# Making an MLP's summed weight factors ahead, behind the mixer blocks' last products

## The chip, the cores and the metric

One core of a Trainium2 chip runs the kernel, in one launch. The metric is the device time of one execution in microseconds, median of several runs; lower is better. Engines go by the profile's names: PE (TensorE), PEld (its weight loads), DVE (VectorE), ACT (ScalarE), POOL (GpSimd) and SP (SyncE, which here issues transfers and nothing else).

## The reference, cut to what matters

```python
def reference(x, meta_tokens, w_in, ...):
    h = jnp.concatenate([meta, x], axis=1)          # 16 + 2048 rows, 1024 wide, float32
    for i in range(DEPTH):                          # DEPTH = 1
        xn = rmsnorm(h, norm_mix_w[i])
        z, xbc, dt_raw, u_s5, gates = jnp.split(xn @ w_in[i], IN_SPLITS, axis=-1)
        y_a = ssd_branch(z, xbc, dt_raw, ...)       # chunked state-space scan, 16 heads
        y_b = s5_branch(u_s5, ...)                  # S5 scan, then y @ w_glu, val * sigmoid(gate)
        g_a, g_b = jnp.split(jax.nn.sigmoid(gates), 2, axis=-1)
        h = h + (g_a * y_a + g_b * y_b) @ w_out[i]
        hn = rmsnorm(h, norm_mlp_w[i])
        h = h + jnp.square(jax.nn.relu(hn @ w_ff_in[i])) @ w_ff_out[i]   # 1024 -> 4096 -> 1024
    return rmsnorm(h, final_norm_w)[:, N_META:]
```

## The kernel before, in words

Every product in float32 is made of three products of a rounded part ("h", "high") and a remainder ("l", "low"): `mm3` (L243 to L245) does high by high, high by low and low by high. So each operand has to be split first: ACT copies it rounded, DVE or POOL subtracts the copy from it.

**Mixer blocks.** The 2048 rows go in four blocks of 512 (`for b in range(NB)`). A block runs through "units" of weights, 1 MB each when split: 16 for the convolved inputs and 16 for the gates of the SSD part, 8 for the mixing gates (`gb`), 8 for `w_glu` and 8 for `w_out`. `rhs_group` takes units one by one, does 24 matmuls for each, and calls `evac` for the results of the last one. Three buffers hold units (`NWU`): `get` issues a unit's load when the unit two before it begins. In block 0 a unit comes raw from the inputs by SP's queue, is split by ACT and POOL (L216, L217) and is stored to DRAM by SP (L225); in blocks 1 to 3 POOL's queue reads it split (`wu<-wsd`, L227). The last two parts of a block are the GLU products (four groups of two units; `evac_glu`, L1261 to L1266, takes the results with ACT, DVE and POOL) and the output products (two groups of four; `evac_out`, L1296 to L1301, adds x and stores h to DRAM). Beside them DVE and ACT make the next block's normalized rows (L261 to L277), and in the last block the MLP's first rows. Memory of the block's SSD part (`ssd%d`) is given back before the GLU part's pool (`glu%d`) is opened.

**The MLP** multiplies by a scheme of seven products in place of eight for each 2 by 2 block of matrices (Strassen's, in Winograd's form). Rows go in three blocks of 768, 768 and 512 (`FB`), each through eight steps (`di`). A step has 28 products: twice seven for `w_ff_in` (`ff_in`) and twice seven for `w_ff_out` (`ff_out`), each with a weight factor. Of the seven factors of a group, three are quarters of the weights as they are and four are sums of quarters.

Class `Weights` supplies the factors. In the first block `make` loads a group's two raw tiles by SP (512 KB each), lets POOL add up the four sums (L1366 to L1369 and L1380 to L1383), and `weight` splits each factor (copy by ACT, L1341; subtraction by DVE or POOL as the string `ENG` says, L1342) into a tile `wc` and stores it to DRAM (`wcd<-wc`, L1343). Three tiles `wc` (`wcs`) and one factor ahead of the product (`AHEAD`) are all there is in that block: a tile comes free when its product and its store are done. In the second and third block `read` fetches the factors from DRAM by POOL's queue (`wc<-wcd` and `wr<-wcd`, L1352) into those tiles and four more.

**Order.** Engines run their queues in order. A planner sets that order: it simulates the program and gives an engine the instruction that is ready, in program order among those that are. `tc.issue_after(mm)` puts what is written under it behind the product `mm`, for instructions of that product's engine, TensorE. A `pool` is a stack of memory on one side of the chip's SBUF: tiles of a new pool wait for the tiles that had the same memory.

Of the kernel before, what the change touches and what calls it, by code (L numbers as in the profile page):

```python
# [9 lines left out]
F32 = mybir.dt.float32  # L10
F32R = mybir.dt.float32r
# [24 lines left out]
NWC = 5  # L36
NWU = 3
NJK = 1
AHEAD = 1
NRAW = 4  # L40
FPACE = 2
# [85 lines left out]
def _body(ctx, tc, d, out):  # L127
# [759 lines left out]
        return t  # L887


    xp = pool("xn", stack=xp_st)  # L890

    def load_x(pl, r0, L, src):
# [193 lines left out]
    for b in range(NB):  # L1086
# [166 lines left out]
            xn = make_xn(gp, b + 1, xp)  # L1253
        mh = gp.tile([P, 8, TB], F32R, name="mixh")
        ml = gp.tile([P, 8, TB], F32R, name="mixl")
        for q in range(4):
            n = q // 2

            def evac_glu(c, p):
                th = gp.tile([P, 256], F32, name="gth", tag="gth", bufs=2)  # L1260
                S.activation(th, p[:, 256:512], AF.Tanh, scale=0.5)  # L1261
                V.scalar_tensor_tensor(th, th, 1.0, p[:, 0:256], op0=ALU.add, op1=ALU.mult)
                o = (q % 2) * 256
                V.scalar_tensor_tensor(th, sgbs[n][:, c, o:o + 256], 1.0, th, op0=ALU.add, op1=ALU.mult)
                ma = mixA[:, c, q * 256:(q + 1) * 256]
                G.tensor_tensor(ma, ma, th, op=ALU.add)  # L1266
            rhs_group([(b, U_GLU + q * 2 + i) for i in range(2)], y5h, y5l, evac_glu)
            if q % 2 == 0:
# [10 lines left out]
        if b == NB - 1:  # L1279
            y5_st.close()  # L1280
            mp_st.close()
            xp_st.close()
            cm_st.close()
            fw = pool("mlpw")
            hp = pool("mlpx", stack=hp_st)
            hn = x_factors(hp, FB[0][1] // 2)
            rows = ff_norm(split_into(hn), lambda nm: ff_raw(fw, nm),
                           lambda nm: ff_sum(fw, nm).rearrange("p (f l) -> p f l", f=4), bank, NE[0],
                           FB[0][0], FB[0][1] // 2, 1)
            for _ in rows:  # L1290
                pass
        for n in range(2):
            def evac_out(c, p, n=n, b=b):
                r0 = b * TB + c * P
                xr = gp.tile([P, 512], F32, name="xr", tag="xr", bufs=2)
                nc.sync.dma_start(xr, d["x"][r0:r0 + P, n * 512:(n + 1) * 512])  # L1296
                V.tensor_tensor(xr, xr, p, op=ALU.add)
                nc.sync.dma_start(h2d[r0:r0 + P, n * 512:(n + 1) * 512], xr)
                jk = gp.tile([P, 512], F32, name="jk", tag="jk", bufs=2)
                i = b * NC4 + c  # L1300
                S.activation(jk, xr, AF.Square, accum_out=ssh[:, n, i:i + 1])  # L1301
            rhs_group([(b, U_OUT + n * 4 + i) for i in range(4)], mh, ml, evac_out)
        if b < NB - 1:
            V.tensor_tensor(ssh[:, 0, b * NC4:(b + 1) * NC4], ssh[:, 0, b * NC4:(b + 1) * NC4],
                            ssh[:, 1, b * NC4:(b + 1) * NC4], op=ALU.add)
            row_scale(ssh[:, 0, b * NC4:(b + 1) * NC4], rsh[:, b * NC4:(b + 1) * NC4], NC4)
        g_st.close()
        if b < NB - 1:
            y5_st.close()
# [13 lines left out]
    class Weights:  # L1323
# [14 lines left out]
        def weight(self, w, eng, n, i):  # L1338

            t = wcs[0].tile([P, 2, n, 512 // n], F32R, name="wc", tag="wc", bufs=wcs[1])  # L1340
            S.copy(t[:, 0], w)  # L1341
            (V if eng == "v" else G).tensor_tensor(t[:, 1], w, t[:, 0].bitcast(F32), op=ALU.subtract)  # L1342
            nc.sync.dma_start(wcd[i], t.rearrange("p a k n -> p (a k n)").bitcast(F32))  # L1343
            return t

        def read(self):
# [6 lines left out]
                    yield t.rearrange("p (a k n) -> p a k n", a=2, k=4 if j < 14 else 2)  # L1353

        def make(self):
            for di in range(ND):
                for half in range(2):
                    c = 2 * di + half
                    wa, wb = ff_raw(fw, "w1a"), ff_raw(fw, "w1b")
                    nc.sync.dma_start(wa, d["w"][U_FFI + 2 * c])  # L1360
                    nc.sync.dma_start(wb, d["w"][U_FFI + 2 * c + 1])
                    a11, a12, a21, a22 = [x.rearrange("p (a k n) -> p a k n", a=2, k=4)[:, i]
                                          for x in (wa, wb) for i in range(2)]
                    s2, s3, s1, s4 = [ff_sum(fw, nm).rearrange("p (k n) -> p k n", k=4)
                                      for nm in ("s2", "s3", "s1", "s4")]
                    G.tensor_tensor(s1, a21, a22, op=ALU.add)  # L1366
                    G.tensor_tensor(s2, s1, a11, op=ALU.subtract)
                    G.tensor_tensor(s3, a11, a21, op=ALU.subtract)
                    G.tensor_tensor(s4, a12, s2, op=ALU.subtract)  # L1369
                    for j, (w, e) in enumerate(zip((a11, s2, s3, a12, s1, a22, s4), ENG[half])):  # L1370
                        yield self.weight(w, e, 4, di * 28 + half * 7 + j)
                for n in range(2):
                    b1, b2 = ff_raw(fw, "w2a"), ff_raw(fw, "w2b")
                    nc.sync.dma_start(b1, d["w"][U_FFO + 4 * di + n])
                    nc.sync.dma_start(b2, d["w"][U_FFO + 4 * di + 2 + n])
                    b11, b12, b21, b22 = [x.rearrange("p (k a n) -> p k a n", k=2, a=2)[:, :, i, :]
                                          for x in (b1, b2) for i in range(2)]
                    t3, t1, t2, t4 = [ff_sum(fw, nm).rearrange("p (k n) -> p k n", k=2)
                                      for nm in ("t3", "t1", "t2", "t4")]
                    G.tensor_tensor(t3, b22, b12, op=ALU.subtract)  # L1380
                    G.tensor_tensor(t1, b12, b11, op=ALU.subtract)
                    G.tensor_tensor(t2, b22, t1, op=ALU.subtract)
                    G.tensor_tensor(t4, b21, t2, op=ALU.subtract)  # L1383
                    for j, (w, e) in enumerate(zip((b11, t3, b21, t4, t1, t2, b22), ENG[2 + n])):
                        yield self.weight(w, e, 2, di * 28 + 14 + n * 7 + j)

        def take(self):
            ahead = AHEAD if wcs[0] is fw and self.n == 0 else NRAW + wcs[1] - 2
# [373 lines left out]
```

## Time and profile before

| | us |
|---|---|
| median of 3 runs | 3317.12 (3313.74 to 3323.17) |
| the profiled execution's own time | 3315.93 |
| its span, first to last instruction | 3314.2 |
| PE busy | 3087.5 (93%) |
| DVE, POOL, ACT busy | 2119.2, 1417.8, 1227.8 |

In the profile's 40 slices of 83 us each (each digit is the busy share in tenths; PEclk the granted clock of TensorE, DMA the share of the 16 DMA engines), the mixer blocks fill slices 2 to 22, the MLP's first block 23 to 29:

```profile
PE   7989889998999999998999889898979999989998
DVE  8689999526844476426764577667675555475555
POOL 3356566523522244213442465665652222243343
PEclk9999989999999999999999999999999999999999
DMA  6376665775555654565756767777788888889998
```

A busy PE is not PE at its peak, and idle time of an engine that nothing waits for costs nothing; what counts is where PE waits.

### The profile page before, as it was taken

The page shows a single profiled execution, that of the slowest core. Times are in us where ns is not written, and L with a number is a line of the kernel's source. Part 1 is how long each engine was busy: PE and PEld are TensorE (multiplying, and loading weights), DVE is VectorE, ACT ScalarE, POOL GpSimd, SP SyncE. Part 2 cuts the span into 40 slices and gives each one's busy share as a digit, 9 for nine tenths or more (in the row PEclk, how much of TensorE's full clock was granted, in tenths as well). Part 3 has the DMA queues.
Part 4 walks back from the last instruction along what each step waited for, and adds up shares of the span by engine and source line. Part 5 has one row for each costly group of instructions (what it writes and reads, how often), then busy time and mean ns, then how long its engine had stood idle before and what let it go on. Part 6 is the DMA issues. An engine that isn't in the chain of part 4 may idle for free. (4 is left out here: it accounts for less than half of the span.)

```text
span 3314.2 us, 50076 instructions
## 1 busy us (share of the span) xinstructions
PE 3087.5 (93%) x18353; PEld 2747.0 (83%) x18353; DVE 2119.2 (64%) x4364; ACT 1227.8 (37%) x2569; POOL 1417.8 (43%) x1736
## 2 busy tenths in 40 slices
PE   7989889998999999998999889898979999989998
PEld 6678777887888778876788788888879999989998
DVE  8689999526844476426764577667675555475555
ACT  5354444434422443324433443334442121142222
POOL 3356566523522244213442465665652222243343
PEclk9999989999999999999999999999999999999999
DMA  6376665775555654565756767777788888889998
GB/s 225 117 220 172 186 168 170 280 248 185 171 197 187 220 156 168 204 229 179 226 174 210 275 254 268 261 272 267 268 292 282 248 248 247 247 286 369 360 358 279
DMA packets 299493, 776.56 MB, mean 234 GB/s; under 512 B 94736, under 2 KB 136848, under 8 KB 270448
## 3 DMA queue, kind: packets, MB, share of 16 engines
q0 software_dynamic: 88832, 411.21, 37.3%
q1 hardware_dynamic: 207808, 360.93, 33.0%
q8 instruction: 146, 2.39, 0.3%
q10 hardware_dynamic: 2608, 1.22, 0.1%
q14 instruction: 99, 0.81, 0.1%
HBM read 560.48 MB, written 214.88 MB: 234 GB/s over the span
## 5 line engine op out<-in xcount | busy, mean ns | idle before, releaser
L1501 DVE TENSOR_TENSOR acc<-acc,p 128x512 f32<-128x512 f32 x330 | 225.8, 684 | 167.0 <-PE p L245 164.8
L243 PE MATMUL pd<-hnh,wc 128*128 128x384 f32 (+1 forms) x896 | 291.2, 326 | 30.9 <-DMA wc<-wcd 20.6
L243 PE MATMUL pd<-wu,xnh 128*128 128x512 f32 x768 | 310.9, 405 | 4.0 <-DMA wu<-wsd 3.1
L245 PE MATMUL pd<-wu,xnl 128*128 128x512 f32 x768 | 310.5, 405 | 0.0
L244 PE MATMUL pd<-wu,xnh 128*128 128x512 f32 x768 | 309.5, 403 | 0.0
L245 PE MATMUL pd<-hnh,wc 128*128 128x384 f32 (+1 forms) x896 | 290.0, 327 | 14.2 <-DVE wc L1342 11.7
L244 PE MATMUL pd<-hnl,wc 128*128 128x384 f32 (+1 forms) x896 | 290.1, 324 | 0.0
L227 POOL DMA_DIRECT2D wu<-wsd x168 | 96.0, 572 | 374.2 <-PE pd L245 309.0
L243 PE MATMUL pd<-xnh,wu 128*128 128x512 f32 (+1 forms) x640 | 232.1, 363 | 9.0 <-DMA wu<-wsd 8.9
L1352 POOL DMA_DIRECT2D wr<-wcd x227 | 121.1, 534 | 273.7 <-PE pd L245 135.0
L244 PE MATMUL pd<-xnl,wu 128*128 128x512 f32 (+1 forms) x640 | 230.2, 360 | 0.0
L245 PE MATMUL pd<-xnh,wu 128*128 128x512 f32 (+1 forms) x640 | 229.9, 360 | 0.0
L1352 POOL DMA_DIRECT2D wc<-wcd x221 | 117.4, 531 | 254.5 <-PE pd L245 136.6
L243 PEld LDWEIGHTS pd<-hnh,wc 128*128 128x128 f32 x896 | 172.1, 192 | 36.4 <-ACT hnh L990 12.2
L749 DVE SCALAR_TENSOR_TENSOR cacc<-craw,conv,cacc 128x512 f32<-128x512 f32 (+1 forms) x192 | 172.1, 897 | 31.8 <-ACT cacc L746 27.1
L245 PEld LDWEIGHTS pd<-hnh,wc 128*128 128x128 f32 x896 | 172.1, 192 | 20.8 <-DVE wc L1342 15.0
L217 POOL TENSOR_TENSOR wu<-wst,wu 128x1024 fp32r<-128x1024 f32 x56 | 137.6, 2458 | 90.7 <-ACT wu L216 85.6
L243 PEld LDWEIGHTS pd<-wu,xnh 128*128 128x128 f32 x768 | 146.8, 191 | 34.9 <-DMA wu<-wsd 4.0
L245 PEld LDWEIGHTS pd<-wu,xnl 128*128 128x128 f32 x768 | 147.2, 192 | 31.6
L244 PEld LDWEIGHTS pd<-wu,xnh 128*128 128x128 f32 x768 | 147.1, 191 | 31.0 <-issue 0.2
L244 PEld LDWEIGHTS pd<-hnl,wc 128*128 128x128 f32 x896 | 172.2, 192 | 0.0
L243 PEld LDWEIGHTS pd<-xnh,wu 128*128 128x128 f32 x640 | 125.2, 196 | 26.1 <-issue 10.8
(1012 smaller groups left out, 9984.0 us busy)
## 6 DMA issues: line engine op xcount, KB each, us to landing
wu<-wsd POOLq DMA_DIRECT2D x168, 1024.0 KB, 5.2
wr<-wcd POOLq DMA_DIRECT2D x227, 512.0 KB, 5.0
wcd<-wc SPq DMA_DIRECT2D x224, 512.0 KB
wc<-wcd POOLq DMA_DIRECT2D x221, 512.0 KB, 5.5
wsd<-wu SPq DMA_DIRECT2D x56, 1024.0 KB
wst<-in_w SPq DMA_DIRECT2D x60, 512.0 KB
csb<-csd SPq DMA_DIRECT2D x16, 1024.0 KB
xt<-in_x SPq DMA_DIRECT2D x28, 512.0 KB
```

Of the source, the lines that this page charges most:

```text
L217: eng.tensor_tensor(t[:, 1], raw, t[:, 0].bitcast(F32), op=ALU.subtract)
L227: nc.gpsimd.dma_start(t, wsd[u - U_XBC])
L243: T.matmul(ps, lh, rh, start=first, stop=False, skip_group_check=open_)
L244: T.matmul(ps, lh, rl, start=False, stop=False, skip_group_check=open_)
L245: return T.matmul(ps, ll, rh, start=False, stop=last, skip_group_check=open_).ins
L749: V.scalar_tensor_tensor(acc[:, :n], raw[:, k:k + n], conv[:, mt, k:k + 1], acc[:, :n], op0=ALU.mult, op1=ALU.add)
L1352: nc.gpsimd.dma_start(t, wcd[di * 28 + j])
L1501: V.tensor_tensor(o, o, pv, op=ALU.add)
```

## The change

30 of the 32 groups have their four sums made, split and stored to DRAM in the mixer blocks: `EARLY` has the numbers of groups for each block, 8, 9, 9 and 4. `ff_early` opens a pool for each block on the right side, beside the GLU part's, with two raw tiles, three sums and two split tiles. After each unit of the GLU and output products (in the last block of the GLU products alone) `early_step` writes two or three pieces of it; a piece is a sum (by DVE in block 0, by POOL in the others), its split (ACT and DVE) and its store (SP). In the MLP's first block, `make` still loads the raw tiles of each group and splits the three quarters, now all with DVE; the four sums it reads back by POOL's queue into the three tiles `wc`. The last two groups are made as before.

```diff
+EARLY = (8, 9, 9, 4)
...
+    def ff_split(t, w, eng, i):
+
+        S.copy(t[:, 0], w)
+        eng.tensor_tensor(t[:, 1], w, t[:, 0].bitcast(F32), op=ALU.subtract)
+        nc.sync.dma_start(wcd[i], t.rearrange("p a k n -> p (a k n)").bitcast(F32))
+
+    def ff_early(pl, groups, eng):
+
+        def load(g):
+            wa, wb = [pl.tile([P, D], F32, name=nm, tag="er", bufs=2) for nm in ("era", "erb")]
+            ff_load(g, wa, wb)
+            return wa, wb
+        raw = load(groups[0])
+        for n, g in enumerate(groups):
+            v, m = ff_pieces(g, *raw)
+
+            def room(nm):
+                return pl.tile([P, 512], F32, name=nm, tag="es", bufs=3).rearrange("p (k n) -> p k n", k=m)
+            for j, w in ff_sums(g, v, room, eng):
+                t = pl.tile([P, 2, m, 512 // m], F32R, name="ew", tag="ew", bufs=2)
+                ff_split(t, w, V, g * 7 + j)
+                if j == (6 if m == 4 else 3) and n + 1 < len(groups):
+                    raw = load(groups[n + 1])
+                yield
...
+        early = ff_early(pool("early%d" % b, stack=e_st, side="right"), range(g0, g0 + EARLY[b]), G if b else V)
+        slots = 8 if b == NB - 1 else 16
+        early_n = [0, 0]
+
+        def early_step(mm):
+            early_n[0] += 1
+            want = -(-early_n[0] * EARLY[b] * 4 // slots)
+            with tc.issue_after(mm):
+                while early_n[1] < want:
+                    early_n[1] += 1
+                    next(early, None)
...
-            rhs_group([(b, U_GLU + q * 2 + i) for i in range(2)], y5h, y5l, evac_glu)
+            rhs_group([(b, U_GLU + q * 2 + i) for i in range(2)], y5h, y5l, evac_glu, step=early_step)
...
-            rhs_group([(b, U_OUT + n * 4 + i) for i in range(4)], mh, ml, evac_out)
+            rhs_group([(b, U_OUT + n * 4 + i) for i in range(4)], mh, ml, evac_out, step=early_step if b < NB - 1 else None)
...
+            for g in range(32):
+                wa, wb = ff_raw(fw, "wa"), ff_raw(fw, "wb")
+                ff_load(g, wa, wb)
+                v, m = ff_pieces(g, wa, wb)
+                a11, a12, a21, a22 = v
+                ws = {0: a11, 3: a12, 5: a22} if m == 4 else {0: a11, 2: a21, 6: a22}
+                early = g < sum(EARLY)
+                if not early:
+                    ws |= dict(ff_sums(g, v, lambda nm: ff_sum(fw, nm).rearrange("p (k n) -> p k n", k=m), G))
+                for j in range(7):
+                    if j in ws:
+                        yield self.weight(ws[j], "v" if early else ENG[g % 4][j], m, g * 7 + j)
+                        continue
+                    t = wcs[0].tile([P, D], F32R, name="wc", tag="wc", bufs=wcs[1])
+                    nc.gpsimd.dma_start(t, wcd[g * 7 + j])
+                    yield t.rearrange("p (a k n) -> p a k n", a=2, k=m)
```

`ff_sums` holds the same four additions and subtractions as before, `ff_load` the same two loads.

## Rows read from the trace of the kernel before

**Rows 1.** The page: the span, and each engine's busy time.
```profile
span 3314.2 us, 50076 instructions
PE 3087.5 (93%) x18353; PEld 2747.0 (83%) x18353; DVE 2119.2 (64%) x4364; ACT 1227.8 (37%) x2569; POOL 1417.8 (43%) x1736
```
**Rows 2.** Timeline of PE, first products of steps: start, us, engine, line, tiles.
```profile
1863.83 0.34 PE L243 MATMUL pd<-hnh,wc 128*128 128x384 f32 x1
1939.02 0.44 PE L243 MATMUL pd<-hnh,wc 128*128 128x384 f32 x1
...
2368.43 0.44 PE L243 MATMUL pd<-hnh,wc 128*128 128x384 f32 x1
2431.31 0.34 PE L243 MATMUL pd<-hnh,wr 128*128 128x384 f32 x1
...
2524.64 0.34 PE L243 MATMUL pd<-hnh,wr 128*128 128x384 f32 x1
...
2883.61 0.34 PE L243 MATMUL pd<-hnh,wr 128*128 128x384 f32 x1
```
**Rows 3.** Stretches: PE, PEld, DVE, ACT, POOL busy (instructions), PEclk, DMA share, GB/s.
```profile
1939.00:2368.00 429.00, 384.83 (x2521) 369.42 (x2520) 303.99 (x420) 169.01 (x312) 265.27 (x193) 0.97 0.74 266
2524.00:2883.00 359.00, 358.13 (x2522) 356.87 (x2521) 196.06 (x336) 72.64 (x144) 101.88 (x180) 1.00 0.82 246
```
**Rows 4.** PE's waits, 1864 to 2431: us in total, times, longest.
```profile
PE p L243 <- DVE acc L1501: 14.8, 9, 2.7
...
PE pd L245 <- DVE wc L1342: 11.7, 9, 1.9
PE p L244 <- POOL wc L1342: 10.1, 9, 2.2
```
**Rows 5.** Groups, 1864 to 2431: busy us, mean ns | idle before, releasers.
```profile
L1342 DVE TENSOR_TENSOR wc<-s,wc 128x512 fp32r<-128x512 f32 x39 | 39.0, 1001 | 36.1 <-ACT wc L1341 32.2 <-DMA wcd<-wc 2.8 <-DMA w1b<-in_w 0.5
L1341 ACT CAST wc<-s 128x512 fp32r<-128x512 f32 x62 | 38.4, 619 | 44.9 <-DMA wcd<-wc 33.0 <-PE py L245 8.3 <-PE pd L245 3.2
...
L1381 POOL TENSOR_TENSOR t<-w2a 128x512 f32<-128x512 f32 x16 | 25.2, 1574 | 1.3 <-DVE wc L1342 1.3
...
L1369 POOL TENSOR_TENSOR s<-w1a,s 128x512 f32<-128x512 f32 x15 | 19.3, 1288 | 4.8 <-DVE wc L1342 4.8
...
L1342 DVE TENSOR_TENSOR wc<-w1a,wc 128x512 fp32r<-128x512 f32 x15 | 10.3, 687 | 8.2 <-ACT wc L1341 8.2
```
**Rows 6.** Line L1352, the factors' reads, 2492 to 2945 (second block).
```profile
DMA to landing us min/median/max: 3.4/4.6/8.1
```
**Rows 7.** Line L1352, 2990 to 3290 (third block).
```profile
DMA to landing us min/median/max: 3.5/5.8/9.4
```
**Rows 8.** Line L227, the one unit load issued from 1127 to 1129.
```profile
DMA to landing us min/median/max: 14.1/14.1/14.1
```
**Rows 9.** Timelines of SP, POOL and PE around that load.
```profile
1125.29 0.93 SPq L881 DMA_DIRECT2D csb<-csd  x2
...
1127.72 0.58 POOL L227 DMA_DIRECT2D wu<-wsd  x1 [1.44 <-PE pd L245]
...
1141.97 0.47 PE L243 MATMUL pd<-xnh,wu 128*128 128x512 f32 x1 [3.10 <-DMA wu<-wsd]
```
**Rows 10.** Stretches as in rows 3: ends of blocks 1, 0 and 3, and block 2's start.
```profile
965.00:1086.00 121.00, 121.00 (x565) 97.57 (x564) 39.62 (x88) 33.13 (x82) 22.66 (x36) 1.00 0.63 220
1086.00:1134.00 48.00, 48.00 (x223) 39.10 (x222) 20.09 (x52) 22.58 (x42) 14.03 (x29) 1.00 0.65 211
585.00:706.00 121.00, 120.33 (x562) 96.65 (x562) 45.19 (x89) 48.39 (x100) 54.50 (x36) 1.00 0.80 287
...
1733.00:1802.00 69.00, 69.00 (x317) 55.64 (x315) 20.01 (x40) 18.48 (x37) 16.99 (x27) 1.00 0.62 207
```
**Rows 11.** Line L227, all 168 unit loads of blocks 1 to 3.
```profile
DMA to landing us min/median/max: 5.0/5.2/15.1
```
**Rows 12.** Line L1264, the gate products of the GLU part: ns min/median/max.
```profile
L1264 DVE SCALAR_TENSOR_TENSOR gth<-sgb,gth x64: 410/425/2037, 610.5 to 1802.5; 128x256 f32<-128x256 f32 x64
```

More of the change, by code (lines that the diff above doesn't have):

```diff
@@ L887, in decays, with ff_pieces, ff_load @@
         return t
+    def ff_pieces(g, wa, wb):
+        if g % 4 < 2:
+            v = [x.rearrange("p (a k n) -> p a k n", a=2, k=4)[:, i] for x in (wa, wb) for i in range(2)]
+            return v, 4
+        v = [x.rearrange("p (k a n) -> p k a n", k=2, a=2)[:, :, i, :] for x in (wa, wb) for i in range(2)]
+        return v, 2
+    def ff_load(g, wa, wb):
+        di, j = divmod(g, 4)
+        ua, ub = (U_FFI + 4 * di + 2 * j, U_FFI + 4 * di + 2 * j + 1) if j < 2 else \
+            (U_FFO + 4 * di + j - 2, U_FFO + 4 * di + j)
+        nc.sync.dma_start(wa, d["w"][ua])
+        nc.sync.dma_start(wb, d["w"][ub])
@@ new lines, in ff_sums, with tt @@
+    def ff_sums(g, v, room, eng):
+        a11, a12, a21, a22 = v
+        def tt(nm, x, y, op):
+            o = room(nm)
+            eng.tensor_tensor(o, x, y, op=op)
+            return o
+        if g % 4 < 2:
+            s1 = tt("s1", a21, a22, ALU.add)
+            yield 4, s1
+            s2 = tt("s2", s1, a11, ALU.subtract)
+            yield 1, s2
+            yield 2, tt("s3", a11, a21, ALU.subtract)
+            yield 6, tt("s4", a12, s2, ALU.subtract)
+        else:
+            yield 1, tt("t3", a22, a12, ALU.subtract)
+            t1 = tt("t1", a12, a11, ALU.subtract)
+            yield 4, t1
+            t2 = tt("t2", a22, t1, ALU.subtract)
+            yield 5, t2
+            yield 3, tt("t4", a21, t2, ALU.subtract)
@@ L1255, in _body @@
         ml = gp.tile([P, 8, TB], F32R, name="mixl")
+        e_st = ExitStack()
+        g0 = sum(EARLY[:b])
+        early = ff_early(pool("early%d" % b, stack=e_st, side="right"), range(g0, g0 + EARLY[b]), G if b else V)
[8 more added lines that the diff above has]
+                    next(early, None)
         for q in range(4):
@@ L1279, in _body @@
         if b == NB - 1:
+            for _ in early:
+                pass
+            e_st.close()
             y5_st.close()
@@ L1306, in _body @@
             row_scale(ssh[:, 0, b * NC4:(b + 1) * NC4], rsh[:, b * NC4:(b + 1) * NC4], NC4)
+        for _ in early:
+            pass
+        e_st.close()
         g_st.close()
@@ L1340, in weight @@
             t = wcs[0].tile([P, 2, n, 512 // n], F32R, name="wc", tag="wc", bufs=wcs[1])
-            S.copy(t[:, 0], w)
-            (V if eng == "v" else G).tensor_tensor(t[:, 1], w, t[:, 0].bitcast(F32), op=ALU.subtract)
-            nc.sync.dma_start(wcd[i], t.rearrange("p a k n -> p (a k n)").bitcast(F32))
+            ff_split(t, w, V if eng == "v" else G, i)
             return t
@@ L1355, in make @@
         def make(self):
[L1356 to L1385, printed above, removed]
@@ new lines, in make @@
+            for g in range(32):
+                wa, wb = ff_raw(fw, "wa"), ff_raw(fw, "wb")
+                ff_load(g, wa, wb)
+                v, m = ff_pieces(g, wa, wb)
+                a11, a12, a21, a22 = v
+                ws = {0: a11, 3: a12, 5: a22} if m == 4 else {0: a11, 2: a21, 6: a22}
[9 more added lines that the diff above has]
+                    yield t.rearrange("p (a k n) -> p a k n", a=2, k=m)
```

## The prediction

> **What bounds the kernel now.** First the page: TensorE (PE) is busy 93% of a span of 3314.2 us, so what counts is where PE stands idle or runs on a lowered clock [rows 1]. Second, the first products of the MLP's steps [rows 2]: in its first block, steps two to seven take (2368.43 - 1939.02) / 6 = 71.6 us, in the second block (2883.61 - 2524.64) / 6 = 59.8 us, for the same 28 products. The whole first block, 1863.83 to 2431.31, is 567.5 us against 8 x 59.8 = 478.6: **89 us is all that this change can win there**. Third, the two blocks by engine [rows 3]: PE works 90% of the first and all but 0.3% of the second; DVE, ACT and POOL are busy 1.6, 2.3 and 2.6 times as long in the first; the granted clock is 0.97 against 1.00, which at two levels (1.2 and 2.4 GHz) is about 6% of the time at the lower one and a loss of about 2.1 us a step. DMA is at 266 GB/s there, 246 in the second block. Fourth, PE's waits [rows 4]: DVE's additions behind its queue, and splits that come late. So the excess is the making of the weight factors.
>
> **MLP's first block, part by part.** 30 of its 32 groups lose four sums on POOL (1.29 to 1.57 us each) and four ACT copies of 0.62 us with their subtractions [rows 5]. A step keeps 12 raw splits, all with DVE's subtraction now (0.69 us where POOL is idle, 1.00 in the mean beside it), and 12 stores; its other 16 factors are read back by POOL's queue. DMA bytes of a step are the same: 4.2 MB raw, and 28 tiles of 0.52 MB, stored before, read or stored after.
>
> New is **the wait of a read for its buffer**. There are three buffers: product t+3 cannot start before the read that was issued when product t ended has landed. Reads of this size land in 4.6 us (median) at 246 GB/s [rows 6], in 5.8 where the DMA is full [rows 7]. A matmul started 0.15 us after its landing (1127.72 + 14.1 = 1141.82, start 1141.97 [rows 8, 9]); with as much and a bit more for the issue, a read costs about 5.05 us (estimate). A product takes 59.8 / 28 = 2.14 us. So a read's turn of a buffer takes 2.14 + 5.05 = 7.19 us, a raw tile's three products, 6.42 (its copy, split and store, 0.62 + 0.69 + 4.6 = 5.9, fit in). 28 tiles share three buffers: (16 x 7.19 + 12 x 6.42) / 3 = 64.0 us a step. Ends: 59.8 if all landings hide, and with landings of 5.8 (16 x 8.39 + 77.0) / 3 = 70.4. I take 64.0, as the first block's DMA rate is nearer to the second block's.
>
> To that I add 1.9 us of DVE lateness (a step's waits by these rows, [rows 4], are some 5 us; DVE loses two splits and its neighbour on POOL) and 1.0 of lower clock, half of today's: 66.9, 4.7 less than 71.6. The last step already ends on reads, 2431.31 - 2368.43 = 62.9, and keeps that; seven steps win **33 us**, with bounds from 0 to 75.
>
> **The mixer blocks, what is added.** 30 groups: 60 loads of 0.52 MB, 120 sums (32 on DVE in block 0, 88 on POOL), 120 copies, 120 subtractions, 120 stores on SP. A group moves 2 loads and 4 stores, 3.15 MB: 25.2 MB in block 0, 28.3 in blocks 1 and 2, 12.6 in block 3. The marking of these steps as behind a product binds instructions of TensorE only, and the pieces have none: the planner puts them where the pool's memory and its own clock allow, from about the last product of the SSD part, some 20 us ahead of the GLU products, on.
>
> Engines, block 1, 965 to 1086 us [rows 10]: DVE 39.6 us busy of 121, plus 36 x 0.69 to 1.00 = 25 to 36; ACT 33.1 + 36 x 0.62 = 55; POOL 22.7 + 36 x 1.29 to 1.57 = 69 to 79. In block 0 DVE has 45.2 and gets 32 subtractions and 32 sums of 0.69 to 1.00 us: 89 to 109 of 121. All fit; PE waits for nobody there now (121.0 of 121.0), so the cover for the work is PE's own products, and if an evacuation is caught behind a piece, PE waits for it whole.
>
> Queues: SP gets 180 more issues, ahead of which stand loads and stores of x and h. A store waits for its split, and what is queued behind it waits too: in block 0 the unit's raw weight load. POOL's queue issues the mixers' weight loads in blocks 1 to 3, and a sum ahead of one, or one that waits for its raw load, delays it. Such a load lands in 5.2 us [rows 11]; when two loads of 1 MB (csb) ran beside it, it took 14.1 us and PE waited 3.10 us [rows 8, 9], so PE covers about 14.1 - 3.1 = 11.0. The early pieces have at most two stores and two raw loads, 2.1 MB, in flight. By these rows I expect 7 to 10 us, inside the cover but for a few.
>
> The nearest price of a piece for PE is the first MLP block's: the two largest waits for wc, 11.7 + 10.1 = 21.8 us [rows 4], come from 224 splits, 0.10 us each, where PE needs the very piece; here it doesn't, but shares queues with it. 120 x 0.10 = 12 us; bounds 0, and for the DMA the 115 us of the first rival. I add 4 us for block 0, where DVE and DMA are fullest: **+16 us**.
>
> DVE and POOL disturb each other: DVE's gate product takes 0.43 us, up to 2.04 [rows 12], which I put down to POOL's work beside it. The Trainium skill, "SBUF — State Buffer", section "SBUF: two separate sides", says why: they share a port pair under an exclusive lock, and a DVE instruction with two SBUF inputs waits for the whole POOL instruction that reads SBUF. The trace agrees so far as the row's 2.04 us fits a wait behind one POOL instruction. The rule speaks against putting sums on POOL beside DVE's evacuations; by it alone DVE could lose 36 sums' time, 46 to 57 us, in such a block and would still end inside 121, so the sum would be the same, with less margin.
>
> **The sum.** -33 + 16 = -17 us. The profiled execution took 3315.9 us, 1.7 over its span and 1.2 under the median of 3317.1; 3317.1 - 17 = **3300 us**. A measurement here tells about 0.3%, 10 us, from no change.
>
> **Rivals.** *A, slower: the mixers' last stages run out of DMA.* Block 1 moves 220 GB/s x 121 us = 26.6 MB; with 28.3 it is 54.9 MB, at 360 GB/s (266 / 0.74 [rows 3]) 153 us: 32 over. The same for block 2; block 0 has 34.7 + 25.2 MB, 166 us: 45 over; block 3 14.3 + 12.6 in 75 of 69 us: 6. That is 115 us if PE's evacuations stand in order behind the pieces, and none if the pieces can trail into the next block, whose first 48 us have a share of 0.65 [rows 10]. It decides where weight loads land later than 11 us or a trailing piece holds memory that the next block's first tiles need. With a third of it, 38 + 12, less 33: 3334; with all of it 3399. For: the DMA is 63 to 80% taken. Against: both ends have room, and PE's 11 us of cover. The Trainium skill, "DMA: Bandwidth & Descriptors", section "Issuing engines are not separate DMA queues", says that all issuers' transfers interleave on the same 16 engines; by that rule SP's pieces slow POOL's weight loads, as [rows 8, 9] show, and this rival would hold in full.
>
> *B, no gain to speak of: the reads land later in the first MLP block.* Each 0.6 us costs 16 x 0.6 / 3 = 3.2 us a step; at 5.2 us the seven steps win 11 us and with the mixers' 16 the time is 3322; at 5.8 it is 3345. For: raw loads and stores run beside the reads, which they don't in the second block.
>
> *C, the reads hide as in the second block:* the steps come near 61, 74 us won, 3259. Against: three buffers here, seven there.
>
> **How the numbers follow.** Forecast 0.43 (own range 3280 to 3315, about 0.05 of it within 0.3%), A 0.31, B 0.18 (0.13 the same, 0.05 slower), C 0.08 (faster). Faster by over 0.3%: 0.38 + 0.08 = 0.46; the same 0.05 + 0.13 = 0.18; slower 0.31 + 0.05 = 0.36. The range reaches from 3262, which leaves out half of C and the best of the forecast, to 3372, which leaves out the upper third of A.
>
> **What would show it.** Right: steps of 66 to 68 us in the first MLP block, PE's waits there by DMA wc<-wcd in place of splits, POOL's sums gone; the mixers' last stages within 5 us of their length, weight loads landing in 7 to 10 us. Wrong: stages of GLU and output products that grow by 10 us and more with PE waiting for DMA wu or for an evacuation behind a piece (A); read landings over 5.2 us and steps over 70 (B); steps under 63 (C); or a next block that starts with PE waiting for DVE.

## Result and profile after

The change makes the kernel slower: median 3450.4 us (3438.55 to 3468.4, 4 runs) against 3316.9 in runs beside them, ratio 1.0402, 95% interval 1.036 to 1.0443. The profiled execution took 3468.4 us, 18 over the median; its stages stand below beside those of before (3315.9). Line numbers are those of each run's own kernel: in the change `mm3` is L244 to L246, the splits L932 and L933. The page, two lines:

```profile
span 3466.7 us, 50568 instructions
PE 3141.1 (91%) x18353; PEld 2775.8 (80%) x18353; DVE 2182.1 (63%) x4501; ACT 1224.4 (35%) x2569; POOL 1293.0 (37%) x1719
```

PE does the same 18353 products, 53.6 us slower, and stands idle for the rest of the 152.5 us that the span grew. Where that is, comes from PE's timeline. A "stage" here runs from a block's first GLU product to the end of its last output product, a "body" from there to the next stage; a step is the mean of steps two to seven of the MLP's first block. All in us:

| | stages of blocks 0 to 3 | bodies of blocks 1 to 3 | MLP's first block | step | span |
|---|---|---|---|---|---|
| before | 101.5, 99.8, 100.2, 109.4 | 279.7, 275.4, 292.9 | 567.5 | 71.6 | 3314.2 |
| after | 133.0, 126.3, 124.7, 113.7 | 298.7, 292.1, 301.4 | 582.0 | 73.1 | 3466.7 |

So the stages cost 86.8 us, the bodies 47.7 with the 3.5 us ahead of block 0's stage, the MLP's first block 14.5, and the remainder 3.5. Neither half came out as forecast. The stretches (columns as in [rows 3]) answer to [rows 10], in the order block 0's stage, the 48 us behind it, block 1's stage, the 48 us behind it, and to [rows 3], six steps of the MLP:

```profile
608.00:741.00 133.00, 112.24 (x475) 87.06 (x474) 91.10 (x136) 55.41 (x113) 51.10 (x33) 0.88 0.94 361
742.00:790.00 48.00, 39.36 (x161) 31.41 (x162) 16.85 (x40) 16.90 (x29) 6.44 (x16) 0.89 0.68 247
1040.00:1166.00 126.00, 107.67 (x471) 84.61 (x470) 59.09 (x109) 42.37 (x100) 59.56 (x60) 0.93 0.93 335
1168.00:1216.00 48.00, 40.97 (x171) 32.58 (x170) 19.32 (x44) 21.05 (x34) 11.70 (x20) 0.93 0.63 216
...
2075.00:2514.00 439.00, 383.72 (x2524) 363.47 (x2524) 243.00 (x409) 114.91 (x216) 64.63 (x108) 0.99 0.81 259
```

In block 1's stage the DMA's share is 0.93, where the same products before ran at this:

```profile
986.00:1086.00 100.00, 100.00 (x471) 80.63 (x470) 35.75 (x82) 27.27 (x72) 20.46 (x32) 1.00 0.57 199
```

PE now idles 18.3 us of 126 and, with the granted clock at 0.93, needs 7.7 more for the same 471 products. No engine is near full: DVE 59 of 126, POOL 60, ACT 42. The 48 us behind a stage suffer too: PE 39.4 and 41.0 busy, where it had been 47.2 and 48.0 of 48. PE's waits in block 1's stage, and for all unit loads the landing times that answer to [rows 11]:

```profile
PE pd L244 <- DMA wu<-wsd: 12.4, 3, 5.7
PE ntp L274 <- DVE xnl L278: 3.7, 2, 3.2
PE pd L244 <- ACT y5h L1311: 1.9, 1, 1.9
...
DMA to landing us min/median/max: 5.0/6.9/15.6
```

In this stage alone the median landing is 8.6 us, before it was 5.1. The timeline shows the two dearest of these waits, POOL's issues and PE's products:

```profile
1130.15 0.56 POOL L228 DMA_DIRECT2D wu<-wsd  x1 [1.61 <-PE pd L246]
...
1139.92 0.79 PE L244 MATMUL pd<-wu,mixh 128*128 128x512 f32 x1 [4.64 <-DMA wu<-wsd]
...
1148.58 0.57 POOL L228 DMA_DIRECT2D wu<-wsd  x1 [3.62 <-DMA erb<-in_w]
...
1158.24 0.79 PE L244 MATMUL pd<-wu,mixh 128*128 128x512 f32 x1 [5.65 <-DMA wu<-wsd]
```

The first load went out as soon as its buffer came free, took 9.7 us, and PE waited from 1139.92 - 4.64 = 1135.28 on: PE covers 5.1 us of a landing here, just what a landing took before. The second also went out as its buffer came free: PE's last product on that buffer ended at 1148.30, and the 3.62 us that POOL had stood behind a raw load of the pieces ended 0.2 us after that. Its cover is 1152.59 - 1148.58 = 4.0 us.

In block 0's stage, where units come raw by SP's queue, PE waits for other work, most for `yt` (rows that SP loads, ACT changes and PE transposes ahead of the GLU products). Behind that stage PE waits for DVE's `xr`, which takes the last output products and itself stands behind loads of x in SP's queue (PE from 608 to 742 and from 742 to 800, DVE from 735 to 770):

```profile
PE y5p L1308 <- ACT yt L1305: 10.2, 2, 5.8
...
PE pd L244 <- DVE xr L1379: 9.1, 2, 5.2
...
DVE xr L1379 <- DMA xr<-in_x: 12.6, 3, 5.1
```

The pieces themselves, and who waits for what (us, times):

```profile
L932 ACT CAST ew<-s x64: 602/620/634, 601.2 to 1939.6; 128x512 fp32r<-128x512 f32 x64
L933 DVE TENSOR_TENSOR ew<-s,ew x64: 677/693/2830, 602.4 to 1940.2; 128x512 fp32r<-128x512 f32 x64
...
  DMA wcd<-ew: 148.8, 62
```

A split takes DVE 0.69 us; ACT stood 148.8 us waiting for stores of earlier pieces to land: the DMA sets the pieces' pace.

In the MLP's first block PE's waits [rows 4] have changed as forecast, from DVE's and POOL's queues to the reads, and the reads land as in [rows 6]:

```profile
PE pd L244 <- DMA wc<-wcd: 25.3, 19, 4.9
PE p L244 <- DMA wc<-wcd: 24.8, 31, 2.1
PE pd L244 <- DVE ka L1528: 7.6, 7, 1.8
PE p L244 <- ACT wc L932: 4.6, 9, 1.2
PE p L245 <- DVE wc L933: 3.6, 9, 0.7
...
DMA to landing us min/median/max: 3.7/4.6/9.5
```

### The profile page after: what moved, and what is told of

Read it like the earlier page. It is cut to its first block, busy times and chain, and to the rows that moved or that the text cites. A ratio compares the mean times of both kernels' runs of the same rounds, so it can differ in the third digit from the quotient of the medians.

```text
span 3466.7 us, 50568 instructions
## 1 busy us (share of the span) xinstructions
PE 3141.1 (91%) x18353; PEld 2775.8 (80%) x18353; DVE 2182.1 (63%) x4501; ACT 1224.4 (35%) x2569; POOL 1293.0 (37%) x1719
## 5 line engine op out<-in xcount | busy, mean ns | idle before, releaser
L244 PE MATMUL pd<-hnh,wc 128*128 128x384 f32 (+1 forms) x896 | 295.3, 331 | 60.9 <-DMA wc<-wcd 44.0
L244 PE MATMUL pd<-wu,xnh 128*128 128x512 f32 x768 | 317.5, 414 | 4.0 <-DMA wu<-wsd 2.4
L246 PE MATMUL pd<-wu,xnl 128*128 128x512 f32 x768 | 314.9, 410 | 0.0
L245 PE MATMUL pd<-wu,xnh 128*128 128x512 f32 x768 | 314.3, 409 | 0.0
L245 PE MATMUL pd<-hnl,wc 128*128 128x384 f32 (+1 forms) x896 | 292.1, 326 | 0.0
L246 PE MATMUL pd<-hnh,wc 128*128 128x384 f32 (+1 forms) x896 | 291.4, 326 | 0.4
L244 PE MATMUL pd<-xnh,wu 128*128 128x512 f32 (+1 forms) x640 | 235.4, 368 | 21.2 <-DVE xr L1379 11.6
L246 PE MATMUL pd<-xnh,wu 128*128 128x512 f32 (+1 forms) x640 | 232.8, 365 | 0.0
L244 PEld LDWEIGHTS pd<-hnh,wc 128*128 128x128 f32 x896 | 173.5, 194 | 72.4 <-DMA wc<-wcd 25.0
L1453 POOL DMA_DIRECT2D wc<-wcd x120 | 64.1, 534 | 445.9 <-PE pd L246 193.5
L1435 POOL DMA_DIRECT2D wc<-wcd x221 | 118.2, 535 | 252.6 <-PE pd L246 132.5
L244 PEld LDWEIGHTS pd<-wu,xnh 128*128 128x128 f32 x768 | 150.7, 196 | 36.3 <-DMA wu<-wsd 2.8
L246 PEld LDWEIGHTS pd<-wu,xnl 128*128 128x128 f32 x768 | 150.1, 195 | 33.4 <-issue 0.2
L245 PEld LDWEIGHTS pd<-wu,xnh 128*128 128x128 f32 x768 | 150.8, 196 | 31.7 <-issue 0.2
L246 PEld LDWEIGHTS pd<-hnh,wc 128*128 128x128 f32 x896 | 173.6, 194 | 1.7 <-DVE wc L933 1.7
```

What stands on the lines that cost most here:

```text
L244: T.matmul(ps, lh, rh, start=first, stop=False, skip_group_check=open_)
L245: T.matmul(ps, lh, rl, start=False, stop=False, skip_group_check=open_)
L246: return T.matmul(ps, ll, rh, start=False, stop=last, skip_group_check=open_).ins
L1435: nc.gpsimd.dma_start(t, wcd[di * 28 + j])
L1453: nc.gpsimd.dma_start(t, wcd[g * 7 + j])
```

## The experiments

Where a kernel has no pieces or doesn't store them whole, the MLP reads tiles of the input weights in the sums' place (in e4 it reads the raw tiles that were stored), so its output is another. e11 ran ten times and e12 four times, every other one once, so differences of some 10 us between their times say little by themselves; the stages are steadier. Measured, in us:

| | stages 0 to 3 | bodies 1 to 3 | MLP first block, step | time |
|---|---|---|---|---|
| e1 reads alone | 101.5, 99.8, 100.5, 104.2 | 278, 277, 293 | 587.9, 72.8 | 3330.6 |
| e2 pieces alone | 132.6, 124.1, 125.5, 114.4 | 295, 292, 298 | 559.6, 70.6 | 3432.5 |
| e3 no stores | 123.0, 111.7, 121.5, 114.1 | 285, 274, 285 | 575.8, 71.6 | 3384.0 |
| e4 transfers alone | 138.4, 122.8, 126.5, 117.4 | 282, 280, 306 | 579.7, 72.0 | 3440.9 |
| e5 reads, four buffers | 101.6, 100.1, 100.2, 111.7 | | 530.0, 64.5 | 3282.1 |
| e6 reads, five buffers | 101.5, 99.9, 100.2, 103.8 | | 516.6, 60.8 | 3272.4 |
| e7 a third of the pieces | 118.5, 110.3, 109.8, 106.2 | 281, 275, 291 | 577.4, 72.0 | 3359.6 |
| e8 engines alone | 120.7, 119.2, 115.8, 112.3 | 282, 276, 286 | 581.0, 72.7 | 3384.0 |
| e9 engines alone, DVE sums | 120.7, 106.8, 107.7, 104.1 | 280, 277, 289 | 573.2, 71.6 | 3348.0 |
| e10 quarter tiles | 107.2, 105.8, 104.6, 115.6 | 283, 277, 294 | 577.8, 73.1 | 3358.8 |
| e11 before, four buffers | 101.6, 101.6, 100.1, 111.5 | | 579.3, 72.0 | 3328.4 |
| e12 before, five buffers | 101.7, 100.3, 100.3, 102.8 | | 680.4, 83.6 | 3430.8 |
| e13 change, DVE sums | 131.2, 120.7, 123.8, 109.4 | 299, 292, 307 | 587.1, 73.8 | 3460.5 |
| e14 the same, four buffers | 133.2, 121.6, 123.3, 108.7 | 297, 290, 304 | 530.3, 64.6 | 3391.7 |
| e15 third, SSD part | 109.3, 113.2, 100.2, 107.4 | 313, 289, 286 | 578.8, 71.0 | 3384.9 |
| e16 third, last stages | 101.6, 112.5, 109.1, 102.8 | 278, 275, 301 | 577.9, 72.6 | 3352.0 |

The kernel before ran between 3311.3 and 3326.0 beside them. Where no piece runs in them, the stages of blocks 0 to 2 lie between 99.8 and 101.7. Block 3's lies between 102.8 and 111.7, so nothing is read from that one. The MLP's first block, making its factors as before, took 567.5 and 559.6 (before, e2); reading them into three buffers it took 573.2 to 587.9 (the change, e1, e3, e4, e8, e9, e10, e13), so its loss of 14.5 us is known to some 8.

### Each half by itself

*e1*, the mixers as before, the MLP with its reads:

```diff
+    def kept_at(i):
+        g, j = divmod(i, 7)
+        if g < sum(EARLY) and j not in ((0, 3, 5) if g % 4 < 2 else (0, 2, 6)):
+            return d["w"][i % U_END]
+        return wcd[i]
...
-        early = ff_early(pool("early%d" % b, stack=e_st, side="right"), range(g0, g0 + EARLY[b]), G if b else V)
+        early = iter(())
...
-                    nc.gpsimd.dma_start(t, wcd[g * 7 + j])
+                    nc.gpsimd.dma_start(t, kept_at(g * 7 + j))
```

> The pieces are left out of the mixer blocks, and the 120 sums' factors are read from the input weights instead (same size, same tile, values that are not the factors). Theory 1 (the reads lose by themselves, since three buffers cannot cover a landing): the first MLP block takes about 580 us as in the changed kernel, against 567 before, and the whole about 3330 us. Rival (the first MLP block loses only because of what the pieces leave behind): the first block takes 535 to 545 us and the whole 3285 to 3295 us. In both the GLU and output stages go back to 100 us.

*e2*, the pieces as in the change, stored to a place of their own, and the MLP making all its factors:

```diff
-                ff_split(t, w, V, g * 7 + j)
+                ff_split(t, w, V, g * 7 + j, wce)
...
-                early = g < sum(EARLY)
+                early = False
```

> The pieces are made in the mixer blocks as in the changed kernel, stored to a scratch of their own that nobody reads, and the first MLP block makes all its factors as before. If the two halves of the change add up, the whole takes 3317 + 133 - 15 = about 3435 us, the stages of GLU and output products 125 to 133 us in blocks 0 to 2, and the first MLP block 567 us. If they don't (the reads' rows lose because the pieces come late, or the planner orders the blocks otherwise), the sum of this and the run with reads alone misses the changed kernel's time by over 30 us.

Both times as expected (e1's first block 8 us over what was expected, e2's 7 under), and the halves add up: 3330.6 is 12 us and 3432.5 is 114 us over the 3318 of before in that batch, together 126 of the 133 measured. The MLP's reads lose time, not only the mixers.

### The MLP: buffers

*e5* and *e6* are e1 with more tiles `wc`, taken from the raw tiles' memory:

```diff
-    wcs = [fw, 3]        # AHEAD = 1, NRAW = 4
+    wcs = [fw, 4]        # AHEAD = 2, NRAW = 3   (e5)
+    wcs = [fw, 5]        # AHEAD = 3, NRAW = 2   (e6)
```

> The run with reads alone, with four buffers for factors instead of three and factors asked for two products ahead instead of one (three raw tiles instead of four, for the room). Theory 1 (a read's turn of a buffer, 2.1 + 5.1 us, is longer than three products, 6.4, but shorter than four, 8.6): the first MLP block's steps fall from 72.8 to 62 to 65 us, the block to 510 to 530 us. Rival (the reads wait behind other work in POOL's queue and on DVE, whatever the buffers): steps of 69 us and more.

> As the run before with five buffers, three products ahead and two raw tiles. Theory 1: little more to win, steps of 60 to 63 us; if the two raw tiles are too few, DVE's and ACT's splits wait for raw loads and the steps are longer than with four buffers. Rival: as with three, 69 us and more.

Both as the theory of the buffers has it: steps of 64.5 and 60.8. e6's block starts late, though: its first product waits 10.3 us for a split by ACT, and the 516.6 don't hold that. In e5 the reads land later than in the change (median 5.3 us against 4.6) and still cost less. Is it the buffers alone? *e11* and *e12* give the kernel before the same ones.

> The kernel before, with four buffers of weight factors in the MLP's first block in place of three, two products ahead in place of one, and three raw tiles in place of four. Theory 9 (the excess of the first block is lateness that a deeper pipeline takes up, on whichever side the factors come from): steps of 63 to 67 us in place of 71.6, the block 515 to 535, the whole kernel 3270 to 3285, as fast as the reads with four buffers (3282). Theory 10 (the making itself is the bound there, DVE's and POOL's queues, and a raw load with three tiles comes later still): steps of 70 to 74, the block 560 to 590, the whole kernel 3310 to 3340.

> The kernel before, with five buffers of weight factors in the MLP's first block, three products ahead, and two raw tiles. Theory 9 (lateness that a deeper pipeline takes up): steps of 61 to 64 us, the block 500 to 525, the whole kernel 3255 to 3275. Theory 10 (the making is the bound, and with two raw tiles a group's loads wait for the last split of the group before): steps of 72 to 80, the whole kernel 3320 to 3390.

No, theory 10 holds, in e12 beyond its range: e11 is 1.0033 of before (1.0021 to 1.0046), e12 1.0339 (1.0316 to 1.0362). PE's waits in e11's first MLP block begin with DVE's queue, as in [rows 4]:

```profile
PE p L243 <- DVE acc L1501: 45.2, 14, 5.8
PE p L243 <- ACT fs1h L1418: 5.7, 8, 2.3
```

and in e12's, with two raw tiles, with the splits:

```profile
PE pd L243 <- ACT wc L1341: 49.1, 27, 6.6
PE p L244 <- DVE wc L1342: 18.5, 21, 2.5
PE pd L245 <- DVE wc L1342: 18.4, 6, 5.3
```

There the making is the bound, in the change the buffers are. Each of these kernels gives up a raw tile for a buffer; the kernel before with four buffers and all four raw tiles was not run. As they were run, neither remedy by itself wins anything; the two together win 37 us of the first block (530.0 against 567.5), and with five buffers 40, counted from the end of block 3's stage.

### The mixers: engines or transfers

*e3* leaves out the pieces' stores. *e8* leaves out the raw loads too (all sums from the first group's tiles), so that only engine work is left. *e4* leaves out all engine work: the raw tiles are loaded and stored as they are.

```diff
 e3, e8
-                ff_split(t, w, V, g * 7 + j)
+                S.copy(t[:, 0], w)
+                V.tensor_tensor(t[:, 1], w, t[:, 0].bitcast(F32), op=ALU.subtract)
 e8 besides
-                if j == (6 if m == 4 else 3) and n + 1 < len(groups):
-                    raw = load(groups[n + 1])
 e4 (era, erb with four buffers)
-            for j, w in ff_sums(g, v, room, eng):
...
+            for k, j in enumerate((4, 1, 2, 6) if m == 4 else (1, 4, 5, 3)):
+                nc.sync.dma_start(wcd[g * 7 + j], raw[k % 2])
```

> The changed kernel with the pieces' 120 stores left out (their sums and splits are made and dropped; the MLP reads from the input weights). Theory 2 (the DMA engines are full: 3.15 MB a group) expects that 1.05 MB a group fits: stages of 100 to 108 us in blocks 1 and 2. Theory 3 (queues: ACT's copies wait for the landing of stores, and evacuations stand behind them) expects the same 100 to 108, since no store is waited for. Theory 4 (the engines' own work, and DVE and POOL locking each other) expects 115 us and more. The whole by theories 2 and 3: 3340 to 3365 us; by theory 4 over 3390.

> The changed kernel with the pieces' transfers alone: the same 60 loads and 120 stores on SP's queue, the stores taken straight from the raw tiles (four of them instead of two), no sums, copies or subtractions in the mixer blocks. Theory 2 (full DMA engines) expects stages of 120 to 130 us in blocks 1 and 2 as in the changed kernel and a whole of 3420 to 3450 us. Theory 3 (queues behind splits that wait for stores) expects 100 to 108 us there and a whole of 3340 to 3365 us.

> The run without stores, with the raw tiles of a block's first group used for all its groups, so that the pieces load and store nothing more; all sums, copies and subtractions are made (the MLP reads from the input weights). Theory 4 (the engines' own work costs PE): stages of 110 us and more in blocks 1 and 2, as without stores (112 and 121). Theories 2 and 3 (transfers, or queues that wait for transfers): 100 to 104 us, and 103 to 110 in block 0, where DVE is fullest.

e4 came as theory 2 had it, stages of 120 to 130; e8 as theory 4 had it, at 110 and more; e3's time lies between what the theories gave, its block 1 too (111.7), while its block 2 (121.5) is as theory 4 had it. So no single one holds. Each alone is enough: the transfers cost block 1's stage 23 us, the engine work 19, and both 26.5. These are not shares of the 26.5: e4's largest wait there, 8.5 us for `yt`, is none of the change's in that stage. e4's stage of block 1, its share of the DMA at 0.97:

```profile
1024.00:1147.00 123.00, 107.19 (x472) 84.79 (x471) 36.14 (x82) 26.78 (x72) 20.36 (x33) 0.93 0.97 376
...
PE y5p L1304 <- ACT yt L1301: 8.5, 1, 8.5
PE pd L244 <- DMA wu<-wsd: 5.0, 4, 1.8
```

In e8 the share is 0.49; there PE waits for DVE, and DVE's subtractions have a median near 1.2 us:

```profile
PE pd L244 <- DVE gth L1346: 9.3, 2, 5.6
PE pd L244 <- ACT y5h L1316: 2.4, 1, 2.4
...
L957 DVE TENSOR_TENSOR ew<-t,ew x16: 675/1242/2583, 1013.3 to 1074.4; 128x512 fp32r<-128x512 f32 x16
L957 DVE TENSOR_TENSOR ew<-s,ew x15: 676/1183/3571, 1007.0 to 1084.3; 128x512 fp32r<-128x512 f32 x15
```

*e7* makes a third of the pieces, `EARLY = (3, 3, 3, 2)`.

> The changed kernel with about a third of the pieces (3, 3, 3 and 2 groups instead of 8, 9, 9 and 4). Theory 2 (the DMA engines are full): with 9.4 MB instead of 28.3 beside 26.6 MB in 121 us they are not (298 GB/s), and the GLU and output stages of blocks 0 to 2 lose 0 to 4 us each instead of 25 to 31. Theory 3 (each piece costs its waits in the queues): they lose a third, 8 to 11 us each, and the next blocks' starts some 5 us. The whole: 3320 to 3330 us by theory 2, 3350 to 3365 by theory 3.

For the stages of blocks 1 and 2 and for the time the size is what theory 3 gave, and theory 2, a DMA that has to be full first, is off by a factor: a third of the dose costs 17, 10.5 and 9.6 us a stage, at a share of the DMA of 0.71 in block 1's. That is two fifths of the whole dose's cost in blocks 1 and 2 and over half of it in block 0. The next blocks' starts, which theory 3 had at 5 us, don't grow. There is no threshold that only the full dose crosses.

*e9* is e8 with DVE's sums; *e10* is e4 with a quarter of each tile's columns in loads and stores, the same issues in the same order.

```diff
 e9
-        early = ff_early(pool("early%d" % b, stack=e_st, side="right"), range(g0, g0 + EARLY[b]), G if b else V)
+        early = ff_early(pool("early%d" % b, stack=e_st, side="right"), range(g0, g0 + EARLY[b]), V)
 e10, against e4
-                nc.sync.dma_start(wcd[g * 7 + j], raw[k % 2])
+                nc.sync.dma_start(wcd[g * 7 + j][:, :256], raw[k % 2][:, :256])
```

> This kernel makes the pieces in the mixers' last stages with no transfers: the sums and splits are made from the first group's raw tiles, nothing is stored, and the MLP reads the input weights in the sums' place. In e8 the sums of blocks 1 to 3 ran on POOL (block 0's on DVE); here all are on DVE. Theory 5 (POOL's sums hold DVE up, its subtractions take 1.3 us beside them): the splits take 0.7 us again, DVE is busy 39.6 + 72 x 0.69 = 89 us of a stage of some 100, and the second and third stages come to 100 to 106 us (e8: 119 and 116); the whole kernel 3345 to 3360. Theory 6 (the pieces' place: an evacuation that stands behind pieces in DVE's and ACT's queues, whatever POOL does): the second and third stages stay at 115 to 122 like the first (120.7, where POOL makes no sums), or grow, as DVE has 36 instructions more; the whole kernel 3380 or more.

> This kernel is the one with transfers alone, each of its raw loads and stores cut to a quarter of the columns: the same number of issues in the same places of SP's queue, a quarter of the bytes; the MLP reads the input weights in the sums' place. Theory 7 (the bytes: the DMA is full in those stages): the added transfers fall from 28.3 to 7.1 MB a stage, the share of the DMA falls from 0.95 to some 0.8, and the first three stages come to 101 to 107 us (whole tiles: 138, 123, 127); the whole kernel 3330 to 3350. Theory 8 (the place in SP's queue: yt's loads stand behind issues that wait for a landing): the stages keep 115 us or more and PE's waits for ACT yt stay at 8 us or more in each block; the whole kernel over 3380.

Both come out in the main as theories 5 and 7 had it (e10's time 9 us over its range). With 36 instructions *more* on DVE, e9's second and third stages fall from 119.2 and 115.8 to 106.8 and 107.7, 1 to 2 us over the range of theory 5, and the subtractions are back at 0.68:

```profile
L957 DVE TENSOR_TENSOR ew<-t,ew x16: 674/680/693, 1007.6 to 1059.0; 128x512 fp32r<-128x512 f32 x16
L957 DVE TENSOR_TENSOR ew<-s,ew x12: 677/680/962, 1023.2 to 1065.9; 128x512 fp32r<-128x512 f32 x12
```

Block 0's stage, whose sums are on DVE in both, stays at 120.7: there theory 6 holds, POOL makes no sums, and PE's largest wait, 5.4 us, is still for DVE's gate products `gth`. In e10 the stages are 104.6 to 107.2: it is the bytes, not the number and order of SP's issues. Whether the bytes act on the unit loads alone or through SP's queue as well, these two runs don't tell: in block 1's stage SP itself stood 65.0 us for landings of the pieces in e4 and 18.4 in e10. Unit loads land in 5.7 us there (8.7 in e4), at a share of 0.73:

```profile
996.00:1102.00 106.00, 101.12 (x474) 80.90 (x473) 36.08 (x82) 26.58 (x73) 20.60 (x32) 1.00 0.73 244
```

### The two together, the remedies, the place

*e13* is the change with DVE's sums (e9's edit); *e14* adds e5's buffers.

> The change as it stands, with the sums of blocks 1 to 3 on DVE in place of POOL; transfers unchanged. Theory 11 (in the whole change the full DMA sets the length of the second and third stages and POOL's hold on DVE is hidden under it): they stay at 121 to 127 us, like the transfers alone (123 and 127), and the whole kernel comes to 3430 to 3455 (the change: 3450). Theory 12 (POOL's hold on DVE is the larger part there too): they come to 107 to 115 us, and the whole kernel to 3400 to 3425.

> The change with the sums on DVE, and in the MLP's first block four buffers of weight factors, two products ahead and three raw tiles. By e5 the first block's steps come to 64 to 66 us and the block to 528 to 540 (the change: 73.1 and 582), so the whole kernel lies 42 to 54 us under e13. By theory 11 that is 3380 to 3410, by theory 12 3350 to 3380; by either the kernel before (3316) stays faster. The rival, that reads which were stored only a block before come later than reads of the inputs: steps of 68 and more.

e13's stages are those of the transfers alone (120.7 and 123.8, e4 122.8 and 126.5), its time 5 us over the range of theory 11: in the whole change the transfers set the pace and POOL's hold on DVE hardly shows (its subtractions have a median of 0.69 us there). PE's waits in block 1's stage lead with the same loads:

```profile
PE pd L244 <- DMA wu<-wsd: 10.5, 3, 5.2
PE pd L244 <- ACT y5h L1311: 2.3, 1, 2.3
```

e14 gets all that four buffers can give, steps of 64.6 as expected; it lies 69 us under e13, 57 of them in the first block, more than the 42 to 54 that I gave, and is still 76 us slower than before.

*e15* and *e16* make 11 groups early, 6 in block 1 and 5 in block 2, sums on DVE: e16 in the last stages, e15 in the SSD part, from a pool that is opened behind `dts.products()` and closed ahead of `kept`'s rest:

```diff
+                if n >= 4:
+                    next(early, None)
```

> 11 of the 30 groups alone are made early, 6 in block 1 and 5 in block 2, with their sums on DVE, one piece per weight unit in the SSD part of the block (a pool of their own there, from the fifth unit on), and none in the last stages. Theory 13 (the cost belongs to the place: the SSD part has a DMA share of about 0.5 and room on ACT): bodies of blocks 1 and 2 grow by 0 to 8 us each, the last stages stay at 100 us, the MLP's first block is 570 to 580 as with the third in the last stages, and the whole kernel comes to 3320 to 3340. Theory 14 (the cost belongs to the pieces: DVE is 75% busy there and a piece takes it 1.4 us wherever it stands): bodies grow by 15 to 25 us each, and the whole kernel comes to 3350 to 3375.

> The same 11 groups (6 in block 1, 5 in block 2, sums on DVE) in the last stages, where the change has them: the twin of e15. Theory 13 (the place): the second and third stages grow by 10 to 20 us each, and the whole kernel comes to 3345 to 3365, 20 to 35 us over e15. Theory 14 (the pieces): within 10 us of e15.

Both theories fall, that of the place on its far side: e15 is 33 us slower than e16, and slower than either theory had it. Nor is it a clean test of the place: the pieces have no instruction on PE, so the planner moved them, and by the starts of their splits 10 ran in block 0's stage already, 14 in block 1's body, 13 in its stage and 7 in block 2's body (e16: 40 of 44 in the two stages). But these four stretches grew by 8, 33, 13 and 14 us: a piece cost 0.8 to 1.0 us in the stages and 2 in the bodies. As these two were run, the last stages were the better place. In e16 the 44 pieces cost (112.5 - 99.8) + (109.1 - 100.2) = 21.6 us there, 0.5 each, the cheapest of all forms with transfers that were run.

No version of the change reached the kernel before: the best reads (e6, 39.5 us under the run of before beside it) leave the pieces 0.33 us for each of 120, and none with transfers was that cheap. Fewer pieces together with more buffers were not run.

## Why the prediction was wrong

**The mixers' term failed, the forecast of +16 us measured +134.5** in the profiled execution (86.8 in the stages, 47.7 in the bodies), 1.1 us for each of 120 pieces, not 0.10. The step that failed is "the nearest price of a piece for PE is the first MLP block's": that price was read among engines' queues at a DMA share of 0.74; here the pieces' transfers make most of it in the stages (e4, e10, e13). What makes up the bodies' part is shown only in places and stays open.

- *"PE covers about 14.1 - 3.1 = 11.0".* That was one load at one place. In the last stages two loads show covers of 5.1 and 4.0 us, and landings that I expected at 7 to 10 us came at 8.6: inside the supposed cover, outside the true one. The trace of before could have told: the last load of block 1's stage went out at 1073.37, and PE came to its unit 6.7 us later, with no time lost as it landed in 5.5. [Rows 10, 11] said only that landings of 5 are covered there; a cover has to be read in the stage that it is used for.
- *Rival A* was nearest: that the added bytes cost the time, e4 against e10 shows, the same issues with a quarter of the bytes. But a stage loses without a full DMA too: e7, 10 us with loads, stores and engine work at a share of 0.71. Its price by bytes was 32, 32 and 45 us for blocks 1, 2 and 0; the stages grew by 26.5, 24.5 and 31.5, and the bodies behind them by 17, 8.5 and 19. Its upper end gave 3399 with a gain of 33 in the MLP; without that gain it is 3432. I gave it 0.31, and cut the range through its upper third. Its other bound, "none if the pieces can trail into the next block", was wrong: they did trail (17 of the 120 splits start behind their stage, up to 30 us into the next body), and PE stood idle 8.6 and 7.0 us in the 48 us behind stages 0 and 1. The prediction's own sign, "a next block that starts with PE waiting for DVE", came behind block 0: 9.1 us for `xr`. e8, engine work alone, and e4, transfers alone, lengthen the bodies of blocks 1 and 2 by 1 to 4 us, e2 with both by 16 each: as far as these runs tell, it takes pieces that wait for stores. Whether memory that such a piece still holds delays the next block was not tested.
- *The idle time's second price*, the clock, stood in the sum for the MLP alone. In block 1's stage PE's idle 18.3 us came with 7.7 us of slower products at a clock of 0.93.
- *Engines that "all fit".* By busy time they do: DVE 78 of 119 us in e8. But e8 loses 19 us there, as evacuations stand behind pieces that take 1.2 us where DVE takes 0.68 without POOL's sums; and block 0's stage loses 19 with pieces of 0.68 us. The Trainium skill, "SBUF — State Buffer", section "SBUF: two separate sides", tells of such a lock between DVE with two SBUF inputs and POOL; e8 against e9 agrees with it, at 1.24 against 0.68 us. I had written that by that rule "the sum would be the same, with less margin", which counted the engine's time and not who stands behind it. In the change itself it hardly occurs (median 0.69 us), perhaps as the stores space the pieces out; e13 finds little to win there.
- The other cited rule, that all issuers' transfers interleave on the same engines (the Trainium skill, "DMA: Bandwidth & Descriptors", "Issuing engines are not separate DMA queues"), held: unit loads from POOL's queue went from 5.1 to 8.6 us beside SP's pieces.

**The MLP's term failed too: -33 us forecast, +14.5 measured.** The mechanism is right, the three buffers' chain: PE's waits are by DMA wc<-wcd, and with four and five buffers (e5, e6) the steps come as that chain has them. The landing's median, 4.6 us, is right to the tenth. What was mis-sized is the turn. Over the trace's steps a read's turn takes about 8.0 us, not 7.19, and a raw tile's 7.6, not 6.42; (16 x 8.0 + 12 x 7.6) / 3 = 73.1, which has to come out, as the turns are read from the same steps. A chain pays the mean: reads land in 5.0 us in the mean and go out 0.6 to 0.9 us in the mean (depending on where one product is taken to end) behind the product that frees their buffer (median 0.3), where POOL waits for a store's landing or a split. A raw tile waits for its store, its split and for ACT; how much each of these adds is not shown. Over what I had put, that makes 0.8 and 1.2 us a turn, 16 x 0.8 / 3 + 12 x 1.2 / 3 = 9 us a step, against the 2.9 that I had added. Rival B named the loss but put it down to the landing.

So the sum, -33 + 16 = -17, was wrong in both terms and in the same direction. The forecast was faster, the result lies 78 us above the range; the uncertainty that I took from single rows was too small for 180 new transfers in the fullest stretch of the kernel.

## What to carry to other kernels

Work that is moved behind products is not free because engines have idle time there: ask what the stage's *covers* are (how late a load may land before PE waits, read in that very stage), and what the added bytes make of landings and of the issuing queue. Taking work away from a pipeline helps only if the next limit, here the number of buffers, is lifted with it; each of the two alone lost time (e1, e11), both together won 37 us of the MLP's first block. In a chain of buffers use the mean of a turn, with late issues, and not the median of a landing.

## What the runs showed of the hardware

- DVE's subtraction of 128x512 took 0.68 us in the median where POOL makes no sums and 1.18 to 1.24 us, up to 3.57, beside POOL's sums (e9, e8, block 1's stage). Moving 36 sums *onto* DVE made the stages of blocks 1 and 2 shorter by 12 and 8 us.
- A unit load of 1 MB landed in 5.1 us (median) at a DMA share of 0.57, in 5.7 at 0.73, in 8.6 to 8.7 at 0.93 to 0.97 (before, e10, the change and e4, block 1's stage; in e8, with POOL's sums, in 5.6 at 0.49). The highest rate in one of the stages shown was 376 GB/s (e4).
- PE's pauses came with a further loss: in block 1's stage of the change, 18.3 us idle and 7.7 of slower products (granted clock 0.93, so partly at the lower of its two levels, 1.2 and 2.4 GHz).
